# Two decoder layers on one core: 24 products of a tile of ones that nothing reads, and the order a list scheduler then writes

## The chip, the core and the metric

The kernel runs on one core of a Trainium2 chip. A core has five engines with a queue each, worked off in order: TensorE (PE in the profile, with its weight loads as PEld), VectorE (DVE), ScalarE (ACT), GpSimd (POOL) and SyncE (SP), which here issues every transfer. The metric is the device time of one execution in microseconds (us); less is better.

## What is computed

Two layers of a decoder over 256 tokens of width 1024, in float32. Layer 0 mixes tokens by a gated delta rule (8 heads of 128, chunks of 64), layer 1 by sparse attention with a relative-position bias; both also attend to 256 memory tokens, and both end in a gated feed-forward with a short convolution. Cut to what matters here:

```python
for i in range(2):
    h = rms_norm(x, norm_mix_w[i]); mem_n = rms_norm(mem, mem_norm_w[i])
    proj = h @ w_in[i]
    mix = gdn_mixer(...) if i == 0 else nsa_mixer(..., rel_bias)   # gdn: short conv, decay, inverse of a 64x64 triangle, recurrence
    mo = memory_attention(proj[..., mem_columns], mem_n, mem_w_kv[i])
    x = x + concat([mix, mo]) @ w_out[i]
    x = x + conv_glu(rms_norm(x, norm_ffn_w[i]), ...)
return rms_norm(x, final_norm_w)
```

## The kernel before

Activations stand feature-major: `x` is eight tiles of 128 features by 256 tokens (`xall`). A weight matrix is streamed in blocks of 128x128. Each chunk of eight blocks (four for the memory weights) is loaded raw (`wr`, `mr`), rounded to a high part on ScalarE (`wh`, `mh`), and its low part is the difference, made on VectorE or, for the memory weights, on VectorE or GpSimd (`wl`, `ml`); `Weights.prep`, lines 478 to 492. The activations are split the same way (`xh`/`xl`, `memh`/`meml`). A product of a block is then three products of 128x256 on TensorE (`proj`, lines 556 to 566).

The code writes no instruction order by hand. `Sched` (lines 56 to 266) records every operation with a cost in microseconds from `Eng._cost` and with its operands, then a list scheduler plays the five engines forward with these costs, takes at each step the operation that can start first on its engine (ties go to the lower priority number, which is the place in the program), and issues the operations in the order in which it took them. Where an operation may run on VectorE or GpSimd, it also chooses the engine. So a cost or an operation added at one place can alter the order and the engine of many later operations.

The program in the order of its stages, with the names that the rows use:

- Memory keys and values of layer 0: `mem_in(0, ...)` splits the memory tokens (`memh`, `meml`), sums their squares (`sq`, `sqa`), and the first products `pf<-memh,mh` follow (lines 679 to 700, 786 to 803).
- The norm of `x`: sums of squares `sqa`, two products with `ones` that add them over the partitions (`mx<-ones,sqa`), `ms` on VectorE, a power on GpSimd (`rs<-ms,nhalf`), two products with `ident` that spread the result (`mx<-ident,rs`), then the normed `hn`, `xh`, `xl` (`rstd_fin`, lines 638 to 654, and lines 812 to 823). The memory norm goes through the same steps first.
- The delta-rule heads in pairs: projections (`pj<-xh,wh`), convolutions `cy`, the keys `kT`, norms `ss` and `rr`, triangle inverse (`DD`, `tm`, `DX`, `lm`), recurrence (`bv`, `vn`, `AT`, `o`). The layer-1 memory norm (`sq<-mt`, `sqa`) and the remaining memory products fill the gaps.
- The bias of layer 1, recorded after the feed-forward of layer 0 but issued early, since little holds it back: a product `mx<-hot,rbe` (8 heads by 384 distances), its copy `bb` on ScalarE, one transfer that spreads it over 128 rows in DRAM (`sk<-bb`, 1,536 KB), and eight transfers that read it back (`bias<-sk`).
- Output projection and feed-forward of layer 0, then layer 1 to the end.

`ones` is a tile of 128x128 float32 that VectorE fills first of all (line 611). A PSUM tile of the tag `mx` is one of six at most, of eight banks in all (`mx()`, line 544).

Of the kernel before, what the change touches and what calls it, by code (L numbers as in the profile page):

```python
# [19 lines left out]
P = 128  # L20
# [35 lines left out]
class Sched:  # L56
    """Records tile operations, orders them with a list scheduler over the engines, then issues them."""

# [192 lines left out]
    def sooner(self, op, e, eng_t, ready):  # L251
        """Whether engine e would finish op before the other engine that can run it."""
        f = {}
        for x, c in op.alt.items():
            t = max(eng_t[x], op.rt)
            wait = sum((o.alt[x] * 0.5 if o.alt else o.cost) for o in ready[x] if o.prio < op.prio and o.rt <= t)
            f[x] = t + wait + c
        return f[e] <= min(f.values())
# [41 lines left out]
class Sub(Vt):  # L300
    """A part of a whole-kernel tile that has its own dependences."""

# [203 lines left out]
def body(ctx, tc, xT, memT, vecs, consts, rows, relb, w_few, w_in0, w_out0, w_up0, w_dn0, w_in1, w_out1, w_up1, w_dn1,  # L506
# [61 lines left out]
    def proj_t(ws, b0, xs, tag="pj"):  # L568
        """Token-major products: [128 tokens, 256 columns] for both halves of the sequence."""
        ps = [pj(tag), pj(tag)]  # L570
        n = len(xs)
        for k in range(n):
            wh, wl = ws.block(b0 + 2 * k, 2)
            xh, xl = xs[k]
            for t in range(2):
                c = slice(t * P, (t + 1) * P)
                with PE.group():
                    mm(ps[t], xh[:, c], wh, start=k == 0, stop=False)
                    mm(ps[t], xh[:, c], wl, start=False, stop=False)
                    mm(ps[t], xl[:, c], wh, start=False, stop=k == n - 1)  # L580
        return ps

    def proj_few(hl, xs, n):
        """Few columns: both parts of the weights are one stationary operand of 2n columns."""
        ps = pj()
        for k in range(KD):
            xh, xl = xs[k]
            with PE.group():
                mm(ps[:2 * n], hl[:, k], xh, start=k == 0, stop=False)
                mm(ps[:2 * n], hl[:, k], xl, start=False, stop=k == KD - 1)  # L590
        return ps[:2 * n]
# [21 lines left out]
    V.memset(nhalf, -0.5)  # L613
    w0 = Weights(sc, w_in0, 36 * KD, "w", 3)

    def rsq(dst, src, n):
# [54 lines left out]

# [1 line left out]
    kTm, vm = {}, {}  # L673
# [62 lines left out]

# [1 line left out]
    def ffn(layer, w_up, w_dn, rs, xs):  # L738
# [41 lines left out]

    # ================= layer 0 =================
    def x_load(k):
# [5 lines left out]
    for ch in "wmmimmwxxxxsb0v":  # L788
        if ch == "m":
            mts += mem_load(len(mts))  # L790
        elif ch == "w":
            wm0.prep()
        elif ch == "x":
            x_load(xk)
            xk += 2
        elif ch == "i":
            ident = fixed([P, P], "ident")
            SY.dma_start(ident, consts[:, C_ID:C_ID + P])
        elif ch == "s":
            ms0 = mem_in(0, mts)  # L800
            mem_k(0, 0, wm0, *ms0[:2])
        elif ch == "b":
            wba = few_weights(w_few[:, :16 * KD], 16, "wba")
        elif ch == "0":
            w0.prep()
        elif ch == "v":
            vecb = fixed([P, NV - V_GNORM], "vecb")
            cst = fixed([P, C_HOT - C_TRI], "cst")
            SY.dma_start(cst, consts[:, C_TRI:C_HOT])
            SY.dma_start(vecb, vecs[:, V_GNORM:])  # L810
    tri = cst[:, :P]
    acc = None
# [12 lines left out]

    # decay and write strength, token-major [128, tile, head]
    ps = proj_few(wba, hs, 16)
# [75 lines left out]
    def silu(dst, y, src, fast):  # L903
        """silu(y), or twice that from the table that Exp is in."""
        if fast:
# [29 lines left out]
    def gdn_pair(p):  # L935
# [55 lines left out]
        yield  # L991
        # inverses of the 16 x 16 diagonal blocks, one block on each partition
        sl = sc.tile("scl", [4 * US], F32, "scl", 2)
# [31 lines left out]

        # doubling of the diagonal blocks: 16 to 32 over whole chunks, then by blocks of 32 and of 64
        for e in range(2):
# [43 lines left out]
        yield  # L1071
        # chunk recurrence and outputs
        zs = {}
# [78 lines left out]

    # ================= layer 1 =================
    hs, rs, rc = normed(V_NMIX + KD, "col")
    rcs = Sm("rcs", [P, 2], 1)
    V.tensor_scalar(rcs, rc, SCALE, None, op0=OP.mult)

    # relative-position bias tiles
    rbe = Sm("rbe", [33, H], 1)
# [19 lines left out]
    w1 = Weights(sc, w_in1, 24 * KD, "w", 3)  # L1179
    # keys of a group: first half of the sequence (selected, window) and compressed; second half  # L1180
    KC = 2 * P + 16
# [5 lines left out]
    vtok = {}  # L1187
    # windows of the keys and values to compress, both parts of both: one stationary operand of 120 columns
    NW = 2 * G * NCMP
# [47 lines left out]
    for j in range(2):  # L1237
# [19 lines left out]
        else:  # L1257
            # three copies of the values on rows 0, 32, 64, for the three products of the parts
            c3 = K("c3", 1, shape=(P, G, 3, 32))
# [225 lines left out]
```

## Time and profile before

| | |
|---|---|
| time, median of 3 runs (lowest to highest) | 844.68 us (844.47 to 845.36) |
| span of the profiled execution (the page has no other time of it) | 845.3 us |
| TensorE matmul busy | 803.3 us, 95%, 6,645 records |
| VectorE busy | 603.8 us, 71% |
| ScalarE busy | 479.6 us, 57% |
| GpSimd busy | 169.7 us, 20% |
| share of the chain that ended last: TensorE | 73% |
| bytes moved | 137.53 MB, mean 163 GB/s |

The table gives sums over the whole span. TensorE's 95% says that it seldom stands still, and it leaves out at which clock it works: that is seen from the distance of two products of the same shape. A matmul record's length holds a tail that overlaps the next record, so distances between starts are read here, and not lengths. A product of float32 operands (such as those with `ones` or `ident`) appears as two records.

### The profile page before, as it was taken

To read this page: it belongs to the slowest core of one execution; us is meant where nothing else is said; L and a number is where in the kernel's file an instruction comes from. 1 tells how busy PE (TensorE), PEld (TensorE's weight loads), DVE (VectorE), ACT (ScalarE), POOL (GpSimd) and SP (SyncE) were. 2 spreads that over 40 slices of the span, in tenths; PEclk is the share of its full clock that TensorE was granted. 3 is DMA by queue.
4 is the path that set the end of the run, shared out by engine and by line. 5 is a ranking of instruction groups with operands and counts; after the bars stand their busy time and mean duration, and the time that the engine had idled before them with its cause. 6 is when DMAs were issued, how large, how long until landed. Compare 5 with 4: busy or idle time off the path is not lost.

```text
span 845.3 us, 17098 instructions
## 1 busy us (share of the span) xinstructions
PE 803.3 (95%) x6645; PEld 787.7 (93%) x6645; DVE 603.8 (71%) x1243; ACT 479.6 (57%) x995; POOL 169.7 (20%) x273
## 2 busy tenths in 40 slices
PE   6999899999964999999999999999999999999996
PEld 5999899999964999999999999999999999999996
DVE  6999888978604856776766668688687776776552
ACT  6577575667513455655544446599954655555340
POOL 2258553643101111111110130000010211111000
PEclk9999999999995999999999999999999999999998
DMA  8664346334347646665666557722255566666641
GB/s 307 209 236 141 118 115 196 104 100 120 96 64 198 206 125 187 187 192 171 180 200 181 176 166 227 230 79 85 88 175 164 188 176 196 180 196 176 181 144 50
DMA packets 53797, 137.53 MB, mean 163 GB/s; under 512 B 11555, under 2 KB 18772, under 8 KB 53716
## 3 DMA queue, kind: packets, MB, share of 16 engines
q1 hardware_dynamic: 53716, 136.44, 54.4%
q8 instruction: 52, 0.85, 0.4%
q14 instruction: 29, 0.24, 0.1%
HBM read 132.48 MB, written 3.94 MB: 161 GB/s over the span
## 4 chain that ended last, share of the span: by engine, by line
PE 73%; DMA 8%; DVE 7%; POOL 5%; issue 5%; ACT 1%; SPq 0%; POOLq 0%; ACTq 0%; DVEq 0%
PE pj L379 60%; PE mx L379 9%; DMA mr<-in_w_mem 4%; PE pf L379 3%; DVE wl L379 2%; POOL DD L379 1%; POOL tm L379 1%; DMA cd<-scd 1%; POOL sqa L379 1%; DVE DD L379 1%; DVE win L379 1%; DMA wr<-in_w_in 1%; DVE cy L379 1%; DMA ident<-in_consts 1%; ACT wh L379 1%
## 5 line engine op out<-in xcount | busy, mean ns | idle before, releaser
L379 PE MATMUL pj<-xh,wh 128*128 128x256 f32 x1152 | 333.4, 289 | 0.0
L379 PE MATMUL pj<-xh,wl 128*128 128x256 f32 x1152 | 326.4, 283 | 1.1 <-DVE wl L379 1.1
L379 PE MATMUL pj<-xl,wh 128*128 128x256 f32 x1152 | 326.2, 283 | 0.0
L379 DVE TENSOR_TENSOR wl<-wr,wh 128x1024 fp32r<-128x1024 f32 x224 | 275.6, 1236 | 35.5 <-ACT wh L379 34.3
L379 ACT CAST wh<-wr 128x1024 fp32r<-128x1024 f32 x224 | 232.0, 1042 | 34.6 <-DVE wl L379 22.6
L379 PEld LDWEIGHTS pj<-xh,wl 128*128 128x128 f32 x1152 | 220.9, 192 | 1.4 <-DVE wl L379 1.3
L379 PEld LDWEIGHTS pj<-xh,wh 128*128 128x128 f32 x1152 | 221.1, 192 | 0.7
L379 PEld LDWEIGHTS pj<-xl,wh 128*128 128x128 f32 x1152 | 221.1, 192 | 0.2
L379 PE MATMUL pj<-gh,wl 128*128 128x256 f32 x352 | 99.8, 283 | 0.0
L379 PE MATMUL pj<-gl,wh 128*128 128x256 f32 x352 | 99.8, 283 | 0.0
L379 PE MATMUL pj<-gh,wh 128*128 128x256 f32 x352 | 99.8, 283 | 0.0
L379 POOL TENSOR_TENSOR fs<-fs,rs 128x256 f32<-128x256 f32 x44 | 39.6, 899 | 215.5 <-ACT fs L379 207.3
L379 PE MATMUL pj<-mixh,wh 128*128 128x256 f32 x192 | 56.9, 296 | 18.1 <-ACT wh L379 18.1
L379 PEld LDWEIGHTS pj<-gh,wh 128*128 128x128 f32 x352 | 67.7, 192 | 0.0
L379 PEld LDWEIGHTS pj<-gh,wl 128*128 128x128 f32 x352 | 67.7, 192 | 0.0
L379 PEld LDWEIGHTS pj<-gl,wh 128*128 128x128 f32 x352 | 67.7, 192 | 0.0
L379 PE MATMUL pj<-mixh,wl 128*128 128x256 f32 x192 | 55.6, 290 | 0.5 <-DVE wl L379 0.5
L379 PE MATMUL pj<-mixl,wh 128*128 128x256 f32 x192 | 55.6, 289 | 0.0
L379 PEld LDWEIGHTS pj<-mixh,wh 128*128 128x128 f32 x192 | 38.1, 198 | 18.4 <-ACT wh L379 18.3
L379 DVE TENSOR_TENSOR fgr<-pj,rs 128x256 f32<-128x256 f32 x44 | 18.6, 422 | 49.1 <-PE pj L379 46.0
L379 POOL TENSOR_TENSOR sq<-xall 128x256 f32<-128x256 f32 x6 | 8.1, 1354 | 224.5 <-DVE xall L379 224.5
L379 DVE SCALAR_TENSOR_TENSOR fy<-fgr,vecb,fy 128x255 f32<-128x255 f32 x88 | 42.4, 482 | 10.1 <-ACT fy L379 9.6
(314 smaller groups left out, 1397.7 us busy)
## 6 DMA issues: line engine op xcount, KB each, us to landing
wr<-in_w_up SPq DMA_DIRECT2D x88, 512.0 KB, 4.3
wr<-in_w_in SPq DMA_DIRECT2D x60, 512.0 KB, 4.5
wr<-in_w_dn SPq DMA_DIRECT2D x44, 512.0 KB, 4.2
wr<-in_w_out SPq DMA_DIRECT2D x24, 512.0 KB, 4.0
mr<-in_w_mem SPq DMA_DIRECT2D x32, 256.0 KB, 3.9
wr<-in_cw SPq DMA_DIRECT2D x8, 512.0 KB, 4.7
mt<-in_memT SPq DMA_DIRECT2D x8, 256.0 KB, 6.0
sk<-bb SPq DMA_DIRECT2D x1, 1536.0 KB
```

The source lines that it names most:

```text
L379: i = getattr(getattr(nc, self.eng), m)(*[fix(x) for x in a], **{k: fix(v) for k, v in kw.items()})
```

## The change

At line 615 a PSUM tile `busy` and a helper `spin` are added; once, between the first loads and the norm of `x` (line 818 of the new text), `spin(24, len(sc.ops))` records 24 products of `ones` by `ones`, float32, 128x128 by 128, all into `busy`, which nothing reads. Each has the priority of that place in the program and a cost of 0.44 us to the scheduler. The other lines of the diff take out comments and docstrings.

```diff
     V.memset(nhalf, -0.5)
     w0 = Weights(sc, w_in0, 36 * KD, "w", 3)
+    busy = mx()
+
+    def spin(n, at):
+
+        for i in range(n):
+            op = PE.matmul(busy[:, :P], ones, ones, start=True, stop=True)
+            op.prio, op.cost = at, 0.44
...
             SY.dma_start(cst, consts[:, C_TRI:C_HOT])
             SY.dma_start(vecb, vecs[:, V_GNORM:])
+    spin(24, len(sc.ops))
     tri = cst[:, :P]
```

The scheduler sets the 24 products where it reckons TensorE without work. On TensorE at the start of the program, the first rows before (`pf` is the accumulator of the first memory keys):

```order
L379 MATMUL pf_117<-memh_104,mh_99 128x256
L379 MATMUL pf_117<-meml_108,mh_99 128x256
L379 MATMUL pf_117<-memh_104,ml_102 128x256
L379 MATMUL pf_117<-memh_111,mh_99 128x256
L379 MATMUL pf_117<-meml_125,mh_99 128x256
L379 MATMUL pf_117<-memh_111,ml_102 128x256
```

and now:

```order
L379 MATMUL mx_90<-ones_78 128x128 x11
L379 MATMUL pf_131<-memh_114,mh_107 128x256
L379 MATMUL pf_131<-meml_119,mh_107 128x256
L379 MATMUL pf_131<-memh_114,ml_111 128x256
L379 MATMUL mx_90<-ones_78 128x128 x2
L379 MATMUL pf_131<-memh_123,mh_107 128x256
L379 MATMUL pf_131<-meml_137,mh_107 128x256
```

Eleven stand ahead of the first product and two behind the first block; one more stands behind the third block, three behind the fourth, one behind the seventh.

On TensorE at the two norms, before (`rs_49` is the memory norm, `sqa_239` the squares of `x`, `rs_74` the norm of `x`, `pf_241` the second memory keys):

```order
L379 MATMUL mx_213<-ones_78,sqa_188 128x1 x2
L379 MATMUL pf_241<-memh_104,mh_219 128x256
...
L379 MATMUL pf_241<-memh_122,ml_231 128x256
L379 MATMUL mx_259<-ident_90,rs_49_237 128x128 x2
L379 MATMUL mx_265<-ones_78,sqa_239 128x1 x2
L379 MATMUL pf_241<-memh_136,mh_219 128x256
L379 MATMUL pf_241<-meml_145,mh_219 128x256
L379 MATMUL pf_241<-memh_136,ml_231 128x256
L379 MATMUL mx_289<-ident_90,rs_74_279 128x128 x2
```

and now:

```order
L379 MATMUL mx_232<-ones_78,sqa_206 128x1 x2
L379 MATMUL mx_90<-ones_78 128x128 x5
L379 MATMUL mx_270<-ident_92,rs_50_259 128x128 x2
L379 MATMUL mx_90<-ones_78 128x128
L379 MATMUL mx_280<-ones_78,sqa_262 128x1 x2
L379 MATMUL pf_287<-memh_114,mh_235 128x256
...
L379 MATMUL pf_287<-memh_147,ml_252 128x256
L379 MATMUL mx_316<-ident_92,rs_75_302 128x128 x2
```

Nine products of the second keys that stood between the two pairs of norm products now stand behind both; five of the products of ones have their place, and all twelve of the half stand ahead of `mx_316<-ident_92,rs_75`.

On VectorE at the same norms, before and now, the copy-out of the first keys (`kTm`) goes ahead of `ms`, the step that the norm of `x` needs:

```order
L379 TENSOR_TENSOR wl_255<-wr_151,wh_234 128x1024
L379 TENSOR_SCALAR gnw_275<-vecb_186 128x1
L379 TENSOR_SCALAR ms_266<-mx_265 128x2
L379 TENSOR_TENSOR kTm_118<-pf_117,rs_260 128x256
L379 COPY DD_283<-cst_170 32x256
```

```order
L379 TENSOR_TENSOR wl_268<-wr_165,wh_256 128x1024
L379 TENSOR_TENSOR kTm_132<-pf_131,rs_271 128x256
L379 TENSOR_SCALAR gnw_292<-vecb_201 128x1
L379 TENSOR_SCALAR ms_281<-mx_280 128x2
L379 COPY DD_297<-cst_187 32x256
```

It is ahead of the norm by one operation; nothing else differs there.

On GpSimd between the last mask of the first heads (`g`) and the norm `rr` of the second pair, before and now (`sq`, `sqa` are squares and sums of the layer-1 memory norm):

```order
L379 AFFINE_SELECT g_248_1040<-g_247_747 128x256
L379 AFFINE_SELECT g_247_747<-g_247_747 128x256
L379 TENSOR_TENSOR rr_1073<-ss_1049,nhalf_88 128x4
L379 TENSOR_TENSOR sqa_1091<-sqa_1079,sq_1071 128x256
L379 TENSOR_TENSOR rb_1107<-rr_1073,hb_532 128x2
L379 TENSOR_TENSOR rb_1107<-rr_1073 128x2
```

```order
L379 AFFINE_SELECT g_249_1013<-g_248_728 128x256
L379 AFFINE_SELECT g_248_728<-g_248_728 128x256
L379 TENSOR_TENSOR sq_1049<-mt_830 128x256
L379 TENSOR_TENSOR sqa_1063<-sqa_1028,sq_1049 128x256
L379 TENSOR_TENSOR sqa_1082<-sqa_1063,sq_1051 128x256
L379 TENSOR_TENSOR rr_1095<-ss_1075,nhalf_88 128x4
L379 TENSOR_TENSOR sqa_1113<-sqa_1098,sq_1089 128x256
```

Three operations on 128x256 that VectorE did, or that stood elsewhere, are now ahead of `rr`.

Up to `mx<-hot,rbe` TensorE has the same 1,540 products in both programs, in another order, and the 24 beside them now. Behind row 1,500 of 6,128 (some 60 rows past `mx<-hot,rbe`) TensorE's order is the same row for row, and SyncE's from shortly ahead of `sk<-bb` on.

## Rows read from the trace of the kernel before

**Rows 1.** Stretches (us): busy us and instructions by engine, TensorE's granted clock, DMA share, GB/s.

```profile
0.00:25.00 25.00, 16.61 (x67) 14.91 (x68) 16.75 (x42) 16.57 (x33) 6.35 (x10) 1.00 0.90 313
25.00:45.00 20.00, 19.98 (x165) 19.46 (x164) 18.35 (x47) 10.79 (x25) 5.71 (x5) 1.00 0.60 186
...
25.00:229.00 204.00, 198.44 (x1771) 188.84 (x1770) 173.18 (x434) 134.72 (x341) 97.87 (x200) 1.00 0.48 141
...
246.00:265.00 19.00, 0.94 (x4) 0.50 (x2) 1.50 (x2) 3.12 (x5) 0.00 (x0) 0.61 0.52 89
```

**Rows 2.** Timeline of SyncE's queue: start, us, instruction, count.

```profile
228.67 0.80 SPq L379 DMA_DIRECT2D sk<-bb  x1
229.57 12.62 SPq L379 DMA_DIRECT2D mr<-in_w_mem  x2
261.24 3.86 SPq L379 DMA_DIRECT2D bias<-sk  x8
```

**Rows 3.** Timeline at the bias; in brackets idle time before, and its releaser.

```profile
227.33 0.81 PE L379 MATMUL mx<-hot,rbe 33*8 33x384 f32 x2
...
228.18 0.47 ACT L379 COPY bb<-mx 8x384 f32<-8x384 f32 x1 [0.74 <-PE mx L379]
...
264.22 0.58 PE L379 MATMUL pj<-mixh,wh 128*128 128x256 f32 x1 [18.06 <-ACT wh L379]
```

**Rows 4.** Timeline of the start.

```profile
0.83 0.17 DVE L379 MEMSET ones<- 128x128 f32 x1 [0.83 <-PEq L1473]
...
5.72 0.58 PE L379 MATMUL pf<-memh,mh 128*128 128x256 f32 x1 [5.72 <-ACT memh L379]
...
8.76 0.58 PE L379 MATMUL pf<-meml,mh 128*128 128x256 f32 x1 [1.51 <-DVE meml L379]
```

**Rows 5.** Timeline of the two norms, 17 to 22 us.

```profile
16.95 0.75 POOL L379 TENSOR_TENSOR rs<-ms,nhalf 128x2 f32<-128x2 f32 x1
...
17.92 1.22 DVE L379 TENSOR_TENSOR wl<-wr,wh 128x1024 fp32r<-128x1024 f32 x1
18.13 1.05 PE L379 MATMUL mx<-ident,rs 128*128 128x128 f32 x4
18.97 0.85 PE L379 MATMUL mx<-ones,sqa 128*128 128x1 f32 x4
...
19.86 0.16 DVE L379 TENSOR_SCALAR ms<-mx 128x2 f32<-128x2 f32 x1 [0.65 <-PE mx L379]
...
20.10 0.70 POOL L379 TENSOR_TENSOR rs<-ms,nhalf 128x2 f32<-128x2 f32 x1 [2.40 <-DVE ms L379]
...
20.86 1.22 PE L379 MATMUL mx<-ident,rs 128*128 128x128 f32 x4 [0.19 <-POOL rs L379]
...
22.12 0.48 DVE L379 SCALAR_TENSOR_TENSOR hn<-xall,vec,mx 128x256 f32<-128x256 f32 x1 [0.37 <-PE mx L379]
```

**Rows 6.** Timeline of TensorE: neighbouring products of one shape.

```profile
24.44 0.42 PE L379 MATMUL pf<-memh,mh 128*128 128x256 f32 x1
24.65 0.42 PE L379 MATMUL pf<-meml,mh 128*128 128x256 f32 x1
...
26.02 0.28 PE L379 MATMUL pf<-memh,ml 128*128 128x256 f32 x1
26.14 0.28 PE L379 MATMUL pj<-xh,wba 128*32 128x256 f32 x1
...
48.03 0.41 PE L379 MATMUL mx<-ident,kT 128*128 128x128 f32 x2 [0.35 <-DVE kT L379]
48.27 0.38 PE L379 MATMUL mx<-ident,qT 128*128 128x128 f32 x2
```

**Rows 7.** Stretches of one us in TensorE's long wait.

```profile
250.00:251.00 1.00, 0.00 (x0) 0.00 (x0) 0.00 (x0) 0.00 (x0) 0.00 (x0) 0.67 0.43 49
```

**Rows 8.** GpSimd, 60 to 75 us: groups by form, and the timeline's row.

```profile
L379 POOL TENSOR_TENSOR sqa<-sqa,sq 128x256 f32<-128x256 f32 x3 | 4.3, 1422 | 0.1
...
64.43 1.13 POOL L379 TENSOR_TENSOR rr<-ss,nhalf 128x4 f32<-128x4 f32 x1 [3.92 <-DVE ss L379]
```

## The prediction

> **What bounds the kernel now.** I read the stretches first, then the queue of SyncE, then the timeline of TensorE where it waits. By the stretches, TensorE is the bound nearly everywhere: between 25 and 229 us it is busy 198.44 of 204 us, so that it stands still for 5.56 us in all [rows 1]. There are two exceptions. In the first 25 us it is busy 16.61 us only, and 5.72 of the 8.4 idle us lie ahead of its first product, which waits for `memh` [rows 1, 4]. And from 246 to 265 us it hardly works [rows 1].
>
> The second exception fixes the end of the program. At 228.67 us SyncE issues `sk<-bb`; two more loads follow, and then the queue holds the eight `bias<-sk` until 261.24 us, with the weights of the output projection behind them [rows 2]. TensorE's first product after that is at 264.22 us, behind an idle time of 18.06 us [rows 3]. So 845.3 - 228.67 = 616.6 us of the span lie behind the issue of `sk`, and TensorE has run out of other work well before they go on. As both programs hold the same instructions in the same order from some 60 TensorE rows past `mx<-hot,rbe` on, I take these 616.6 us as fixed: **what the change does to the time is what it does to the moment of `sk`.** That moment hangs on TensorE: `mx<-hot,rbe` at 227.33 us stands in line behind 1,540 products, `bb` copies it at 228.18 us, and `sk` goes [rows 2, 3]. The 1,540 are the same now, so three things can move it: the clock of the first 25 us, the 24 products where nothing covers them, and the 5.56 us of waiting after that.
>
> **The clock.** Up to 24.44 us two neighbouring products of 256 columns start 0.21 us apart; at 26.02 us they start 0.12 us apart [rows 6]. The first is 1.2 GHz and the second 2.4 GHz. (The column of the granted clock says 1.00 for the first 25 us all the same; the spacing decides.) What TensorE did before the rise: from 20.86 us on it had no gap. What it did before the fall in the long wait: it had stood still from 246 us, and the granted clock falls inside the stretch 250 to 251 us [rows 1, 7]. A float32 product of 128 columns, two records, costs 0.84 / 2 = 0.42 us at the lower level (two from 18.13 to 18.97 us) and 0.24 us at the upper (48.03 to 48.27 us) [rows 5, 6].
>
> **The change part by part.** *Eleven products at the start.* `ones` is there at 1.00 us [rows 4]. At the lower level they take 11 x 0.42 = 4.6 us and end at 5.6 us, ahead of the 5.72 us at which `memh` comes: cost nothing, covered by that wait. Were the cover gone, 4.6 us. With the first blocks behind them TensorE is busy without a gap from 1.0 to beyond 7 us, longer than the stretch without a gap from 20.86 us that came before the rise in the profile; so I expect the clock up before 8.76 us.
> *Two products behind the first block* (at most 0.84 us) lie in the 1.51 us that end at 8.76 us [rows 4]. *The next five* (one, three, one) cost 1.2 us at the upper level; at that level the 24 products of the first keys take half their time, and they wait for `meml` and `ml` as before, so these lie in waits too. Bounds: nothing to 1.2 us; I take nothing, because all of this ends in the wait for the memory norm.
> *Six at the norms.* The memory norm `rs` is there at 16.95 + 0.75 = 17.70 us, on GpSimd, whatever TensorE does [rows 5]. Five products ahead of it lie in the wait for it. From there at the upper level: two norm products to 18.2, one of ones to 18.4, two sums of `x` to 18.9 us, where before they ended at 18.97 + 0.85 = 19.8 us. That gain does not reach `ms`: VectorE is in `wl` until 19.14 us, and now `kTm` stands ahead of `ms` as well; the row is idle for 0.65 us before `ms` [rows 5], and `kTm`, as 128x256 from PSUM like `hn` at 0.48 us, fills most of it. With `gnw` 0.15 us of `ms`'s own size behind it, `ms` starts at about 19.75 us instead of 19.86: 0.1 us gained. GpSimd's `rs` follows at 20.7 us, and the two norm products cost 0.48 instead of 0.84 us. **So `hn` starts some 0.5 us sooner**, and with it the chain over VectorE.
> *TensorE's own lead.* From 18.9 us twelve products of the second keys take 12 x 0.12 = 1.4 us; it waits for `rs` until 20.7, does the norm products to 21.2, then 24 products in 2.9 us: 24.1 us, where the first projection `pj<-xh,wba` stood at 26.14 us [rows 6]. **Lead 2.0 us.**
> *Nine products put behind the norms.* They cost nothing at the upper level (they are inside the 2.9 us); at the lower, see the second rival.
>
> So the sum is between -0.5 us (only the chain's lead counts) and -2.0 us (TensorE's counts). Between 25 and 45 us TensorE is idle for 0.02 us and VectorE for 1.65 us [rows 1]: TensorE is the bound there, and the value is nearer to -2.0 us. It is lost to the extent that TensorE then waits longer for VectorE and GpSimd than 5.56 us. The scheduler set `kT` and its like earlier in both queues, so I leave these waits as they are. **845.3 - 2.0 = 843.3 us for the profiled execution; the runs' median is 0.6 us below that span, so 842.7 us.**
>
> The Trainium skill (TensorE: Matmul & The Clock Gate, "A second HAM failure mode: psum-queue depth-cycling") speaks against the step of the clock: it describes a kernel in which short idle times of TensorE between groups of products made the clock go up and down, and the time was lost in that. Between 8.8 and 17.7 us this kernel has such short idle times, and more of them at the upper level. The trace of before bears it out only in part: from 25 to 229 us TensorE has its 5.56 us of short waits and the granted clock reads 1.00 throughout [rows 1], but it is far busier there. By that rule the time would be that of the second rival, 845.7 us.
>
> **The rivals.** *The lead is eaten.* At 48.03 us TensorE already waits 0.35 us for `kT` from VectorE [rows 6]; if VectorE's chain is only 0.5 us ahead there, TensorE's 2.0 us become 0.5, and the time is 844.7 - 0.5 = 844.2 us. For it: VectorE is busy 18.35 of 20 us [rows 1], almost as much as TensorE. Against it: part of its own idle time there is waiting for TensorE.
> *The products do not keep the clock up.* Either the clock does not rise by 18 us, or it has fallen again. Then the norm products end at 18.5, the product of ones at 19.0, the sums at 19.8 us, twelve products take 2.5 us until 22.3, and `mx<-ident,rs`, now behind all twelve, starts there instead of at 20.86 us: `hn` is 1.5 us later, TensorE's sum of work 0.4 us (one product of ones without cover). 845.1 to 846.2 us, say 845.7.
> *A queue is written worse (slower).* GpSimd stood idle for 3.92 us before `rr` of the second pair of heads [rows 8]; now one square and two sums of the layer-1 memory norm stand ahead of it, 3 x 1.42 = 4.3 us by the nearest row [rows 8]. If their operands are there when the masks end, `rr` is 0.4 us late; if they come as late as `ss` itself, 4.3 us, and the queues of VectorE and TensorE hold what needs `rr` in line. The whole price gives 844.7 - 2.0 + 4.3 = 847.0 us. It decides against the change from a delay of 3.7 us on (2.0 of lead and 1.7, which is 0.2%).
>
> **How the numbers follow.** 0.2%, 1.7 us, is about what a measurement of this kernel can tell from no change: 843.0 to 846.4 us count as no change. Chances: the forecast, 842.7 us, 0.42; the lead eaten, 844.2 us, 0.27; the clock not kept, 845.7 us, 0.12, of which 0.02 above 846.4; the queue, about 847 us, 0.19. Faster 0.42, within 0.2% 0.27 + 0.10 = 0.37, slower 0.19 + 0.02 = 0.21. Downwards the range takes in that TensorE's waits also shrink, by 2.3 of their 5.56 us: 840.4 us. Upwards it takes in the full price of the queue and stops at 847.2 us; beyond the two ends I leave 0.06 and 0.12. The likeliest case alone: 841 to 843 us.
>
> **What would show it.** Right: eleven products from about 1.0 us, neighbouring products 0.12 us apart before 18 us, `pj<-xh,wba` at about 24 us, TensorE's idle time from 25 us to `sk` near 5.6 us, `sk` near 226.7 us, and 616 us from there to the end. The lead eaten: the same start, but idle time of 7 us or so, and `kT` near 47.5 us. The clock not kept: 0.21 us apart at 20 us and `hn` behind 23 us. The queue: `rr` at 66 us or later with `sq` and `sqa` ahead of it. All of it would be wrong if the 616.6 us behind `sk` moved.

## The result, and the profile after

The changed kernel takes 853.22 us (median of 4 runs, 852.65 to 853.99), the kernel before, run beside it, 845.02 us (844.47 to 846.02). The ratio is 1.0089, 95% interval 1.0073 to 1.0106: **slower by 0.9%**, some 7.5 us, where I had forecast 842.7 us. Three things are to be read from the profile after: what the products do at the start, when `sk` goes, and what lies between.

The start of TensorE's timeline (start, us, instruction, count, idle time before and what ended it), as [rows 4 to 6] of before:

```profile
1.05 4.30 PE L379 MATMUL mx<-ones 128*128 128x128 f32 x22 [1.05 <-DVE nhalf L379]
5.91 0.38 PE L379 MATMUL pf<-memh,mh 128*128 128x256 f32 x1 [0.56 <-ACT memh L379]
...
6.65 0.28 PE L379 MATMUL pf<-memh,ml 128*128 128x256 f32 x1
6.77 0.61 PE L379 MATMUL mx<-ones 128*128 128x128 f32 x4
...
18.07 0.42 PE L379 MATMUL pf<-memh,ml 128*128 128x256 f32 x1
18.28 0.42 PE L379 MATMUL pf<-memh,mh 128*128 128x256 f32 x1
...
24.35 0.28 PE L379 MATMUL pj<-xh,wba 128*32 128x256 f32 x1
```

The eleven products (22 records) are over before `memh` comes, and from 6.65 us neighbouring products start 0.12 us apart: TensorE runs at 2.4 GHz some 18 us sooner than before. From 18.07 us, behind a wait of 1.68 us for the memory norm that ended at 16.62 us, they are 0.21 us apart again, until 21.6 us. The first projection stands at 24.35 us, where it stood at 26.14 us [rows 6]: a lead of 1.79 us. So far the change does what it says.

SyncE's queue, as [rows 2]:

```profile
238.51 0.80 SPq L379 DMA_DIRECT2D sk<-bb  x1
239.43 12.60 SPq L379 DMA_DIRECT2D mr<-in_w_mem  x2
271.08 3.75 SPq L379 DMA_DIRECT2D bias<-sk  x8
```

`sk` goes 9.84 us later than before (228.67 us). The stretches between, as [rows 1] (length, then busy us and instructions of TensorE, its weight loads, VectorE, ScalarE, GpSimd, then TensorE's granted clock, DMA share, GB/s):

```profile
24.35:237.17 212.82, 198.77 (x1753) 189.85 (x1750) 172.87 (x431) 132.64 (x339) 98.92 (x195) 0.98 0.46 136
25.00:238.51 213.51, 199.46 (x1754) 189.93 (x1753) 173.03 (x432) 132.48 (x341) 99.56 (x200) 0.98 0.46 135
42.00:45.50 3.50, 3.50 (x19) 3.50 (x19) 3.46 (x11) 2.91 (x6) 0.00 (x0) 0.52 0.44 119
210.00:216.50 6.50, 6.17 (x27) 5.88 (x28) 3.10 (x9) 1.56 (x6) 2.02 (x2) 0.54 0.50 161
```

The first stretch runs from the first projection to `mx<-hot,rbe`, which `sk` waits for. Before, it was 201.19 us long with 195.63 us busy:

```profile
26.14:227.33 201.19, 195.63 (x1753) 186.68 (x1750) 170.73 (x428) 132.64 (x337) 96.44 (x199) 1.00 0.48 143
```

Now it is 212.82 us with 198.77 us busy. So TensorE stands still 14.05 us and not 5.56 us (+8.49), and it is busy 3.14 us longer, since two pieces of it run at half clock. 8.49 + 3.14 - 1.79 of lead = 9.84 us. The two longest of the new waits end ahead of those two pieces:

```profile
39.99 0.38 PE L379 MATMUL pj<-xh,wl 128*128 128x256 f32 x1 [2.25 <-DVE wl L379]
...
210.33 2.07 PE L379 MATMUL mx<-DX,lm 128*128 128x128 f32 x8 [3.48 <-POOL DX L379]
```

Smaller new ones: 1.58 us for `kT` at 79.9 us (before 0.28), 1.66 us for `DX` at 103.2 us (before 0.25), 1.11 us for `kd` at 165.8 us (before none). None of them is at a product of ones.

### The profile page after: what moved, and what is told of

The parts are those of the page before. It is cut to its first block, busy times and chain, and to the rows that moved or that the text cites. A ratio compares the mean times of both kernels' runs of the same rounds, so it can differ in the third digit from the quotient of the medians.

```text
span 851.9 us, 17219 instructions
## 1 busy us (share of the span) xinstructions
PE 806.2 (95%) x6693; PEld 791.1 (93%) x6693; DVE 604.5 (71%) x1243; ACT 478.4 (56%) x995; POOL 171.7 (20%) x273
## 4 chain that ended last, share of the span: by engine, by line
PE 72%; DVE 9%; DMA 8%; POOL 5%; issue 5%; ACT 1%; SPq 0%; POOLq 0%; DVEq 0%
PE pj L379 60%; PE mx L379 9%; DMA mr<-in_w_mem 4%; PE pf L379 3%; DVE wl L379 2%; POOL tm L379 2%; DMA cd<-scd 2%; POOL DD L379 1%; DVE cy L379 1%; DMA scl<-LL 1%; DVE tm L379 1%; DVE win L379 1%; DVE DX L379 1%; DMA scd<-DD 1%; DVE DD L379 1%
```

## Experiments

Ratios are to the kernel before, run on the same chip beside each group; the interval is 95%. A profile shows one execution.

### The order and the products, each alone

The scheduler takes the 24 products into its reckoning at 0.44 us each, and so re-orders some 430 rows of TensorE, and many of VectorE and SyncE. The first run keeps that order and issues no product:

```diff
-            op.prio, op.cost = at, 0.44
+            op.prio, op.cost, op.skip = at, 0.44, True
...
-            op.run(self.nc)
+            if not getattr(op, 'skip', False):
+                op.run(self.nc)
```

> The 24 products are planned for at 0.44 us each, so that every engine has the order of the changed kernel, but none of them is issued. Theory O (the order costs the time): the waits of the changed kernel stay (2.25 us at 40 us, 3.5 us at 210 us), and its 1.8 us lead at the start is lost or not, so 852 to 856 us, ratio 1.008 to 1.013. Rival P (the products themselves cost it, by what they do to the clock or to the first real products): without them the time is that of the kernel before, 844 to 846 us, ratio 1.00. Rival S (either alone costs little, only both together do): under 850 us.

Measured: 855.93 us, ratio 1.0120 (1.0102 to 1.0139). The second issues the products at the same places, outside the scheduler, and keeps the old order:

```diff
+AT = {0: 11, 1: 2, 3: 1, 4: 3, 7: 1, 10: 5, 13: 1}
...
+            if op.eng == "tensor":
+                n = AT.get(k, 0)
...
+                    for i in range(n):
+                        self.nc.tensor.matmul(b.real[:, :P], self.ones.real[:], self.ones.real[:], start=True, stop=True)
+                k += 1
             op.run(self.nc)
```

> The 24 products are issued at the places of the changed kernel among the first loads (11 ahead of the first real product, 2, 1, 3, 1, 5 and 1 further on), but the planner knows nothing of them: every engine has the order of the kernel before. Theory O: the first real products go at .12 us apart and not at .21, the lead at the first of pj<-xh,wba is 1.5 to 2.0 us, the waits from 25 us to sk stay at 5 to 6.5 us, and the time is 842.5 to 844.5 us, ratio 0.997 to 0.9995. Rival P: 850 us or more, ratio over 1.005. Rival L (the lead is eaten by the weights, which come no sooner): 844.5 to 845.5 us, with the waits from 25 us to sk longer by the lead.

Measured: 843.68 us, ratio 0.9975 (0.9958 to 0.9991). **The order costs the time, the products save some**, and the two make up the whole: 1.0120 x 0.9975 = 1.0095, against 1.0089 for the changed kernel. In the profile of the order alone the long waits stand where they stood, without any product of ones (the profiled execution, 852.07 us, is the quickest of the four):

```profile
40.91 0.39 PE L380 MATMUL pj<-xh,wl 128*128 128x256 f32 x1 [2.15 <-DVE wl L380]
...
210.89 1.16 PE L380 MATMUL mx<-DX,lm 128*128 128x128 f32 x8 [1.69 <-POOL DX L380]
```

```profile
25.00:236.36 211.36, 197.86 (x1763) 187.22 (x1762) 174.61 (x434) 133.53 (x342) 100.88 (x200) 1.00 0.46 136
```

From 25 us to its `sk` TensorE stands still for 211.36 - 197.86 = 13.50 us, against 5.56 us before and 14.05 us in the changed kernel. The granted clock is 1.00 there, and TensorE is busy no longer than before (198.11 us over the same part): the waits belong to the order, and the 3.14 us more of busy time in the changed kernel to its two pieces at half clock.

In the profile of the products alone the first projection, `sk` and the stretch between are what the prediction wanted, and better. TensorE's row, SyncE's row, and the stretch:

```profile
23.12 0.28 PE L398 MATMUL pj<-xh,wba 128*32 128x256 f32 x1
```

```profile
226.14 0.80 SPq L398 DMA_DIRECT2D sk<-bb  x1
```

```profile
25.00:226.14 201.14, 195.56 (x1744) 185.58 (x1743) 171.30 (x430) 132.94 (x338) 96.14 (x199) 1.00 0.47 143
```

The lead is 26.14 - 23.12 = 3.02 us, and TensorE stands still for 201.14 - 195.56 = 5.58 us behind it, as before (5.56).

Two more runs change one number of the edit. With 21 products at 0.44 us the scheduler finds the old order; from 22 on a new one.

```diff
-    spin(24, len(sc.ops))
+    spin(21, len(sc.ops))
```

> The changed kernel with 21 products and not 24, each still planned for at 0.44 us. With 21 every engine has the order of the kernel before and the products stand where the changed kernel's stand but for the last three; from 22 on the order is a new one. Theory O (the order costs the time, the products save some): 842 to 845 us, ratio 0.996 to 1.000, with the waits of the kernel before behind 25 us. Rival (the planned 0.44 us or the products cost it, whatever the order): 848 to 853 us.

Measured: 843.39 us, ratio 0.9973 (0.9957 to 0.9989). `pj<-xh,wba` stands at 23.48 us, `sk` at 225.80 us. Three products fewer are worth 1.2%, with the tile `busy` and 21 products still there. The other number:

```diff
-            op.prio, op.cost = at, 0.44
+            op.prio, op.cost = at, 0.12
```

> The changed kernel with one number changed: each of the 24 products is planned for at 0.12 us, not 0.44. All 24 then stand ahead of the first real product, and every engine has the order of the kernel before. Theory O (the planned cost re-ordered the work, and the order costs the time): as the kernel with the products in the old order, 842.5 to 845 us, ratio 0.996 to 1.000; the 24 end at 6 to 6.5 us, half a microsecond behind the first data (5.7 us), which the early clock gives back. Rival: 24 products in one row delay the first real ones and the norms by more than the clock gives back: 845.5 to 847 us.

Measured: 847.01 us, ratio 1.0015 (0.9999 to 1.0030): the forecast missed, though the order is the old one, and the time is the rival's, at its upper end. At 0.12 us the scheduler puts all 24 ahead of the first real product, which then starts at 7.78 us and not at 5.76, and none is left for the gaps between 14 and 18 us. Stretches of this run, and then of the run with the products spread, at the same times:

```profile
14.00:18.00 4.00, 3.07 (x14) 2.77 (x15) 3.86 (x9) 1.88 (x4) 2.19 (x3) 0.52 1.04 395
18.00:22.00 4.00, 3.81 (x18) 3.52 (x17) 2.98 (x8) 2.35 (x4) 0.71 (x1) 0.50 1.04 412
```

```profile
14.00:18.00 4.00, 3.73 (x30) 3.35 (x30) 3.86 (x9) 1.71 (x4) 2.07 (x3) 1.00 1.05 398
18.00:22.00 4.00, 3.16 (x27) 2.96 (x26) 4.00 (x11) 3.35 (x7) 0.71 (x1) 1.00 1.03 410
```

In one row the products raise the clock but don't keep it; spread, they keep it. The late start is made up by the sums (`mx<-ones,sqa` at 13.84 us here, at 13.71 us with the products spread), so the lead stands or falls with the clock; that is read from one profile of each. The rest of this profile's loss is a wait of 1.43 us for `DX` at 148.7 us with half clock behind it, which two other profiles of the old order show too (1.58 us in the run with 110 products below, 0.64 us in that with the loads moved) and the rest don't; I don't know its cause.

### The worst places of the new order

At 200 us SyncE has the two 64 KB hops of the last pair of heads, `scd` to DRAM and `cd` back. SyncE's queue after, and then GpSimd's row:

```profile
200.08 0.33 SPq L379 DMA_DIRECT2D scd<-DD  x1
200.50 0.37 SPq L379 DMA_DIRECT2D wr<-in_w_out  x1
201.71 0.38 SPq L379 DMA_DIRECT2D cd<-scd  x1
```

```profile
207.10 3.17 POOL L379 TENSOR_TENSOR DX<-cd,cst 128x256 f32<-128x256 f32 x3 [4.48 <-DMA cd<-scd]
```

The new order has a 512 KB weight transfer between them; before, `cd` followed `scd` directly. `cd` takes 5.3 us to land, GpSimd's three `DX` start at 207.10 us, and TensorE waits for them until 210.33 us. One step moved, in the order that is issued (1639 is that `wr`, 1303 the `cd`):

```diff
+LATER = [(1639, 1639, 1303)]
...
+            if any(lo <= op.i <= hi and not self.ops[after].inst for lo, hi, after in LATER):
+                held.append(op)
+                continue
```

> The changed kernel with one step moved: the 512 KB weight transfer that SyncE issues at 200.5 us, between the two 64 KB hops scd and cd of the last pair of heads, is issued behind cd. Theory D (that transfer holds up cd, which holds up GpSimd's three DX, for which TensorE waits 3.5 us at 210 us, after which it runs at half clock until 216 us): cd lands by 204 us and not 207 us, the wait goes, and the time falls by 3.5 to 6.5 us, to 847 to 850 us. Rival: cd is held up by the transfers that are on their way already, or the weights that come 1.5 us later are waited for instead: 852 to 854 us.

Measured: 850.92 us, ratio 1.0057 (1.0039 to 1.0074). `cd` lands in 2.5 us, and GpSimd's row is

```profile
205.81 2.20 POOL L390 TENSOR_TENSOR DX<-cd,cst 128x256 f32<-128x256 f32 x3 [1.63 <-DMA cd<-scd]
```

TensorE has no wait of over 0.25 us between 185 us and the long wait. The time is 0.32%, 2.7 us, off the changed kernel (each was timed against the kernel before in a group of its own, and the two intervals just touch). The mechanism is shown; the gain is below the 3.5 to 6.5 us that I expected. In the profile `sk` goes at 234.09 us, 4.42 us sooner, but behind `sk` this execution takes 3.2 us longer than that of the changed kernel. Nor is the wait a fixed price: in four more profiles with the weight transfer between the hops (the order alone, and the three runs below that leave it there) `cd` takes 3.5 to 5.7 us to land, and TensorE waits 1.63 to 3.90 us for `DX`.

The wait at 40 us is VectorE's: eleven small gate operations now run ahead of the `wl` that TensorE needs. Moved behind it:

```diff
+LATER = [(161, 171, 270)]
```

> The changed kernel with one step moved: on VectorE the part wl of the weights that TensorE waits for at 40 us (2.25 us) is computed ahead of the eleven small operations zz and ln of the gates, and not behind them. Theory V (VectorE's new order costs the wait and the half clock from 42 to 45.3 us behind it): the wait falls under 0.5 us and the clock stays up, so the time falls by 2 to 4 us, to 849 to 851.5 us. Rival (the time before the second wait at 210 us is slack: what is gained at 40 us is waited away again at kT, DX or sqa): TensorE arrives at 200 us less than 1 us sooner, and the time is 852 to 853.5 us.

Measured: 857.49 us, ratio 1.0117 (1.0087 to 1.0147): no gain, and slower than either forecast. The wait went to the next thing that VectorE owes:

```profile
40.37 0.61 PE L390 MATMUL mx<-gg,cst 128*128 128x16 f32 x2 [2.13 <-DVE gg L390]
```

With the products of `gg` and what hangs on them moved as well:

```diff
+LATER = [(161, 171, 270), (175, 176, 692)]
```

> The changed kernel with the part wl of the weights ahead of the small gate operations on VectorE, and also the two products of gg and what hangs on them behind the last eight-step product pj of that head on TensorE. In the run with wl ahead alone the wait of 2.2 us at 40 us only passed from wl to gg. Theory G (the new order brings the gates forward on VectorE and TensorE, and work that TensorE could do stands behind them): both waits fall under 0.5 us, the clock stays up from 42 to 45 us, TensorE arrives at 60 us 2.5 to 4 us sooner than in the changed kernel, and the time is 847.5 to 851 us. Rival (VectorE's work as a whole is late there, or the lead is waited away again before 200 us at kT, DX or sqa): 851.5 to 855 us.

Measured: 853.54 us, ratio 1.0095 (1.0073 to 1.0116), the time of the changed kernel. TensorE now waits 2.00 us at 44.2 us, for ScalarE's `gc` (the operations that I moved now follow one another in one row, each waiting for the one ahead of it), and the wait for `kT` at 80 us has grown from 1.58 to 2.46 us. Theory G falls as I put it.

At 76 us the trace of after shows VectorE like this, and then GpSimd:

```profile
75.76 2.51 DVE L379 TENSOR_TENSOR tm<-Lb,DD 32x28 f32<-32x28 f32 x1 [0.69 <-POOL DD L379]
```

```profile
75.69 2.53 POOL L379 TENSOR_TENSOR ml<-mr,mh 128x512 fp32r<-128x512 f32 x2
```

An operation of 32x28 takes 2.51 us, over the same time as GpSimd's two `ml`, and `kT` stands behind it. With the two `ml` moved behind the eight `tm` and `DD` that follow on GpSimd, and behind `rr` and one more `DD`:

```diff
+LATER = [(1487, 1487, 473), (1494, 1494, 473)]
```

> The changed kernel with one step moved: GpSimd's two operations ml of 128x512, which in its trace run from 75.7 to 78.2 us while VectorE's small tm (0.17 us elsewhere) takes 2.51 us over the same time, go behind the eight tm and DD that follow on GpSimd. Theory H (VectorE is held while GpSimd works on ml, kT comes late by that, and TensorE waits 1.58 us for kT at 79.9 us): tm takes 0.2 us, kT comes some 2.3 us sooner, that wait falls under 0.4 us, and the time falls by 1 to 2.5 us, to 850.5 to 852.2 us. Rival (what is gained there is waited away behind it, at kT 98.5 or DX 103 us, as it was when the 40 us wait was attacked): the wait at 80 us goes and the time stays at 852.5 to 854.5 us.

Measured: 855.34 us, ratio 1.0098 (1.0064 to 1.0131). The rows are those of theory H, the time is no better than its rival's: `tm` takes 0.18 us and the wait for `kT` falls to 0.30 us, but now TensorE waits for the `ml` itself (VectorE's row, then TensorE's):

```profile
77.50 0.18 DVE L393 TENSOR_TENSOR tm<-Lb,DD 32x28 f32<-32x28 f32 x1 [1.75 <-POOL DD L393]
```

```profile
86.78 0.39 PE L393 MATMUL pf<-ml,memh 128*128 128x256 f32 x1 [1.86 <-POOL ml L393]
```

Both moves that did what they should to a row, together:

```diff
+LATER = [(1639, 1639, 1303), (1487, 1487, 473), (1494, 1494, 473)]
```

> Both moves together: the weight transfer behind cd at 200 us, which alone gave 850.9 us, and GpSimd's two ml later. If the two waits cost independently of one another: 848.5 to 850 us. If the time between 80 and 200 us is slack to what TensorE gains at 80 us: 850.5 to 851.5 us. If the order as a whole could be mended by its two worst places it would come to 846 us or less; I don't expect that.

Measured: 850.10 us, ratio 1.0042 (1.0025 to 1.0059), against 1.0057 with the transfer alone (the intervals overlap) and 1.0098 with the `ml` alone. So one place, the transfer between the hops, is worth some 2.7 us against the changed kernel and 4.7 us (0.56%) against the run with `ml` moved; at the other places that were tried, what is gained is waited away at the next.

A third order, made by planning for 36 products and issuing none (with the `skip` of the first run):

```diff
-    spin(24, len(sc.ops))
+    spin(36, len(sc.ops))
```

> No product is issued, but 36 are planned for at 0.44 us each: a third order, as far from that of the kernel before (about 430 rows of TensorE) as the changed kernel's is, and as far from that too. Theory A (a plan that is made for an idle time which the chip doesn't have is worse whatever it looks like): 850 to 860 us. Rival B (orders scatter about the same time by a few us, and the changed kernel's is a bad draw): 840 to 850 us.

Measured: 850.79 us, ratio 1.0052 (1.0036 to 1.0067), at the border of the two theories. It is slow for another reason: its `pj<-xh,wba` stands at 29.45 us, 3.3 us late, and from 25 us to its `sk` TensorE stands still for 5.49 us only. The delay comes from the norm of `x`, with the products behind it 0.21 us apart from 26.25 to 29.45 us:

```profile
25.34 0.71 PE L380 MATMUL mx<-ident,rs 128*128 128x128 f32 x4 [1.85 <-POOL rs L380]
...
29.45 0.37 PE L380 MATMUL pj<-xh,wba 128*32 128x256 f32 x1
```

Neither theory holds as written: not every wait is worse in an order made for work that isn't there, but both such orders lose, each at a place of its own.

### The long wait

The products keep the clock in the gaps of the start; do they in the wait of 18 us, behind which TensorE runs at half clock for some us? All kernels here have the old order and the products at the start, 843.7 us.

```diff
+FILL = 110
...
+            if op.i == 1642:
+                b = next(t for o in out[out.index(op):] for t in o.allocs if t.cls == "ps")
+                if b.real is None:
+                    b.real = real(b)
+                for i in range(FILL):
+                    self.nc.tensor.matmul(b.real[:, :P], self.ones.real[:], self.ones.real[:], start=True, stop=True)
```

> The old order with the products at the start, and 110 more products of ones ahead of the operation that TensorE waits for from 246 to 264 us, some 13 us of them at 0.12 us each, written to the tile that this operation begins. Theory K (products in a wait keep the clock; behind the 18 us wait TensorE runs at half clock for 3.3 us in some executions and 6.6 us in others): the products behind the wait are 0.12 us apart from the first on, 1.5 to 3.3 us go, and the time is 840 to 842.5 us, ratio 0.993 to 0.997. Rival (the last 4 to 5 us of the wait, which the products don't fill, let the clock fall all the same): 843 to 844 us.

Measured: 848.43 us, ratio 1.0028 (1.0016 to 1.0041), slower. I had sized a product at 0.12 us, the distance of two records; it is two records:

```profile
L281 PE MATMUL pj<-ones x220: 271/275/275, 247.8 to 272.3; 128*128 128x128 f32 x110
```

110 of them took 24.5 us, 0.22 us each, and held the first real product up until 272.33 us, 6.3 us past the moment (35.55 us behind `sk`, as before) at which the wait was over. With 74, written to the same tile:

```diff
-FILL = 110
+FILL = 74
```

> As the run with 110 products in the 18 us wait, now with 74. There each product of ones took 24.48 us / 110 = 0.22 us and not 0.12, so that they ended 6 us behind the moment at which the wait had ended, with the clock up. 74 of them take 16.5 us of a wait of 18.05 us. Theory K: the clock is up from the first real product on, 1.5 to 3.3 us go against the kernel without them (843.7 us), and the time is 840 to 842.5 us. Rival (1.6 us of standing still at the end of the wait let the clock fall): 843 to 844 us, with half clock behind the wait.

Measured: 844.15 us, ratio 0.9978 (0.9965 to 0.9990), no better than without (0.9975). The products end 1.54 us ahead of the weights, a second wait of 0.76 us follows, and then:

```profile
262.00:264.00 2.00, 0.75 (x4) 0.55 (x5) 1.53 (x2) 1.38 (x2) 0.00 (x0) 1.00 0.88 249
264.00:266.00 2.00, 2.00 (x13) 2.00 (x13) 1.85 (x4) 0.80 (x2) 0.00 (x0) 0.65 0.89 235
266.00:268.00 2.00, 2.00 (x12) 2.00 (x11) 1.88 (x3) 1.10 (x2) 1.29 (x2) 0.50 0.98 350
268.00:270.00 2.00, 2.00 (x18) 2.00 (x18) 1.21 (x2) 0.97 (x1) 0.93 (x1) 1.00 0.99 356
```

The clock is still up when the real work begins at 262.49 us, and falls after that, while TensorE is busy. The half clock is put off, not saved.

The wait itself: I took `bias<-sk` for its cause and moved the eight loads 60 us back.

```diff
+LATER = [(2915, 2922, 2130)]
```

> The old order with the products at the start, and SyncE's eight loads bias<-sk, which wait for the 1.5 MB sk until 261 us and hold up all weights behind them, issued behind a weight transfer some 60 us later; the tiles are first read at 546 us. Theory W (the weights behind them are all that TensorE waits for from 246 to 264 us): the wait of 18 us falls to 3 to 10 us, with some of the half clock behind it, and the time is 825 to 837 us, ratio 0.977 to 0.991. Rival (sk fills the DMA engines, and the weights come no sooner): 841 to 844 us.

Measured: 845.01 us, ratio 1.0000 (0.9984 to 1.0016), and the wait is 18.07 us as ever: theory W falls. What holds TensorE is ScalarE, in the trace of before:

```profile
261.88 0.62 ACT L379 CAST mh<-mr 128x512 fp32r<-128x512 f32 x1 [23.22 <-DMA mr<-in_w_mem]
262.40 0.83 ACT L379 ACTIVATE vm<-pf,rs 128x256 f32<-128x256 f32 x2
263.13 1.99 ACT L379 CAST wh<-wr 128x1024 fp32r<-128x1024 f32 x2
```

A cast waits 23.22 us for a 256 KB transfer that is issued behind the 1.5 MB `sk`; the two weight casts behind it need nothing new. With that cast, and the next load of `mr`, moved behind five casts of weights, three of which find their weights there, and the loads `bias<-sk` moved as before:

```diff
+LATER = [(2915, 2922, 2130), (1874, 1874, 1672), (1887, 1887, 1672)]
```

> The old order with the products at the start, SyncE's bias<-sk loads some 60 us later, and one cast of ScalarE (mh<-mr, whose 256 KB transfer is issued behind the 1.5 MB sk and lands at 262 us) and the next mr load moved behind three casts wh<-wr whose weights came before 215 us. Moving the loads alone changed nothing. Theory C (the wait from 246 to 264 us is ScalarE's: three weight casts stand behind one that waits 23 us for a transfer): three chunks of 24 products, 8.6 us of TensorE's work, move into the wait, and the time is 833 to 839 us, ratio 0.985 to 0.992. Rival (VectorE's part wl or the next weights, behind sk too, take the wait over in full): 842 to 844.5 us.

Measured: **837.26 us, ratio 0.9896** (0.9878 to 0.9915). The wait is 10.15 us, and ends with the weights that come behind `sk`:

```profile
262.73 0.58 PE L409 MATMUL pj<-mixh,wh 128*128 128x256 f32 x1 [10.15 <-ACT wh L409]
```

Against the run with the loads alone (1.0000) the cast and the load of `mr` give 1.0%. The cast without the loads `bias<-sk` moved was not run, so how much of the gain needs both is open.

And with 40 products of ones in what is left of it:

```diff
+FILL = 40
...
+            if op.i == 1677:
+                b = next(t for t in op.allocs if t.cls == "ps")
+                for i in range(FILL):
+                    self.nc.tensor.matmul(b.real[:, :P], self.ones.real[:], self.ones.real[:], start=True, stop=True)
```

> The version with ScalarE's weight casts ahead (837.3 us), and 40 products of ones (8.9 us at 0.22 us) ahead of the operation that TensorE then still waits 10.15 us for. Theory K: the half clock from 262.7 to 269.3 us goes, 1.6 to 3.3 us less, 834 to 836 us. Rival: the products end too late or the clock falls all the same: 837 to 839 us.

Measured: **835.05 us, ratio 0.9865** (0.9849 to 0.9881), the quickest version, 10 us ahead of the kernel before. The 2.2 us between the last two are not certain (the intervals overlap), since here too the clock falls some 2 us after the work has begun again.

## Why the prediction was wrong, step by step

*Everything hangs on `sk`.* Right as to the delay: 9.84 us there, 6.6 us in the two profiled spans, 8.2 us in the medians. But the 616.6 us behind it are not fixed, and by the prediction's own sign that is a second error, one that made the loss look smaller: 613.4 us after, 614.2 us with the products alone, 616.6 us again with the transfer moved. Of the 3.2 us between before and after, 0.4 us are the long wait (from `sk` to its end 35.18 against 35.55 us), 1.2 us the moment at which the clock comes back behind it, 1.1 us lie at two products `mx<-wl,win` some 300 us behind `sk`, and the rest in the last microseconds. Stretches of two us from the first product on, before and then after:

```profile
268.00:270.00 2.00, 2.00 (x11) 2.00 (x11) 1.88 (x3) 0.82 (x2) 1.56 (x2) 0.50 0.98 341
270.00:272.00 2.00, 2.00 (x16) 2.00 (x16) 1.23 (x3) 1.05 (x1) 0.64 (x1) 0.80 1.01 365
```

```profile
276.00:278.00 2.00, 2.00 (x13) 2.00 (x13) 1.72 (x6) 1.60 (x3) 0.16 (x1) 0.63 0.80 250
278.00:280.00 2.00, 2.00 (x20) 2.00 (x18) 2.00 (x2) 0.30 (x1) 1.92 (x2) 1.00 0.84 283
```

Before it comes back 6 to 7 us behind the first product at 264.22 us, after 3 to 4 us behind that at 273.69 us. The order of the work there is the same in both, and the run with the transfer moved has the new order and 616.6 us, so I don't put this down to the change.

*Eleven products under cover, the clock up before 8.76 us.* Right: 1.05 to 5.35 us (I had 5.6), up at 6.65 us.

*The other thirteen at no cost.* Right: with the products alone nothing is lost, and beside the run with all 24 in front it shows that these keep the clock in the old order. I had not given them that work.

*`hn` 0.5 us sooner, TensorE 2.0 us ahead at `pj<-xh,wba`.* `hn` starts at 21.69 us against 22.12 [rows 5], 0.43 us; the lead is 1.79 us, with 3.5 us of half clock in it, 3.02 us where the clock stays. Right in kind, and the term was rather too small.

***The waits behind 25 us stay at 5.56 us.* This is the step that failed.** I wrote that the scheduler "set `kT` and its like earlier in both queues" and left the waits alone. I had looked at the re-ordered queues only for single steps that were late, and priced the products by what they take on the chip, not by what they do to the plan. They are 10.6 us to the scheduler, and the order it makes for them waits 14.05 us, 13.50 us where none of them is issued. With the old order the step holds to 0.02 us. The scheduler does not see the loss: played through with its own costs, the new order has `sk` at 194.99 us and the old one at 195.18 us, so that to its reckoning the two are as good as equal. That `cd` lands later behind the weight transfer, or that `tm` is held beside `ml`, is not in its costs (it has `cd` land 2.1 us after its issue in either order).

*The rivals.* "A queue is written worse" is the mechanism, and holds nearly all that I gave the side that came; place and price were wrong. I had it on GpSimd at `rr` of the second pair with 4.3 us; there `rr` starts at 65.61 us, 1.2 us later [rows 8], after waiting for `ss`. The price that could be traced is 2.7 us of time (4.42 us at `sk` in the profile), at SyncE's transfer between two hops; no other single place that was tried gave any back. I gave it 0.19. "The clock not kept" came in part, from 18.07 to 21.6 us, and behind the two long waits; in the run with the transfer moved, with the same wait of 1.68 us for the memory norm, the granted clock from 18 to 22 us is 1.00 (0.57 in the changed kernel). The rule of the Trainium skill that I weighed there (TensorE: Matmul & The Clock Gate, "A second HAM failure mode: psum-queue depth-cycling") has the clock going up and down with short idle times; the trace after agrees at 18, 42 and 210 us (granted clock 0.57, 0.52 and 0.54 behind waits of 1.68, 2.25 and 3.48 us), and not between 47 and 209 us, where waits of 1.1 to 1.7 us stand and the granted clock is 1.00.

What stays open: which of the remaining waits of the new order (5 us by the ratio 1.0057) come from VectorE's order and which from TensorE's. Neither order was tried by itself.

## What to carry to other kernels

Work that nothing reads is not free where a list scheduler sees it. Issue it outside the plan, at places read from a profile, and compare the order of the real work before and after; here 21 products left it alone and 22 did not. A lower price kept the order too, but put all the products in one place, where they gave nothing (ratio 1.0015). When an edit re-orders hundreds of rows, ask first which transfers, casts and chains have something new between their steps, and do not carry the old idle time over as a constant. And look behind the queue that seems to block: moving the loads `bias<-sk` gave nothing, moving one cast that stood ahead of ready ones, and the load behind it, as well gave 1%.

## What the runs showed of the hardware that I had not expected

A float32 product of ones by ones of 128 columns leaves two records: 24.5 us / 110 = 0.22 us at full clock. Such products take the clock up by themselves: behind 24 of them in one row the first real products stand 0.12 us apart.

The clock can fall after work has begun again: in the run with 74 products TensorE stood still for 1.54 and 0.76 us, went on at full clock at 262.49 us, and the stretch from 266 us ran at half clock although it was busy throughout. And a wait as long as another need not have it: behind the 2.15 us at 40.9 us in the run of the order alone the granted clock stays at 1.00, behind 2.25 us in the changed kernel it is 0.52.

A small operation of VectorE can take as long as what GpSimd has under way: 2.51 us for `tm` beside 2.53 us of `ml`, 0.18 us once `ml` is elsewhere. The Trainium skill names such a contention, without a time (GPSIMD Engine Reference, "1. Specifications": the two engines share their interfaces to SBUF, and contend when an instruction of VectorE has two inputs from there, as `tm` has). So an operation given to GpSimd to spare VectorE can cost VectorE its whole length.

A transfer of 64 KB issued behind one of 512 KB took 3.5 to 5.7 us to land in five profiles, 2.5 us without it ahead.
